# A hybrid encoder block on one core: mixer modulation in sets 1024 columns wide, one gate set placed earlier

## The chip, the cores and the metric

One core of a Trainium2 chip runs the whole layer in one launch. The metric is device time in microseconds: 1252.6 is the median of 3 runs of the kernel before (1247.02 to 1254.28).

## The reference, cut to what matters

256 tokens of width 2048 pass through one layer, all in float32. c is a single vector.

```python
c_act = silu(c)
mod = c_act @ ada_w + ada_b              # 2048 x 12288, one row
shift_a, scale_a, gate_a, shift_f, scale_f, gate_f = split(mod, 6)
h = rmsnorm(x, norm1_w) * (1.0 + scale_a) + shift_a
proj = h @ w_in                          # 2048 x 5184
q_r, k_r, v_r, g_r, cq, ckv, k_rope = split(proj, ...)
# retention heads from q_r, k_r (rotary), v_r, gated by silu(g_r)
# attention heads from the latents cq, ckv (w_uq, w_ukv) and k_rope (rotary)
x = x + gate_a * (concatenate([ret_out, mla_out]) @ w_o)
h = rmsnorm(x, norm2_w) * (1.0 + scale_f) + shift_f
x = x + gate_f * ((silu(h @ w_gate) * (h @ w_up)) @ w_down)
return rmsnorm(x, final_norm_w)
```

## The kernel before

**Weights.** All weight matrices lie in one DRAM stream, cut into loads in the order in which they are used, mostly [128 x 1024] float32 (512 KB). SP issues every DMA. A load lands in a staging slot: the ring `stg` has 6, and until the attention tiles are opened (`att_open`) a second ring `stgx` in the pool `early` adds `DEEP` = 9. A weight load is then split (`split_weights`): ScalarE casts it to `whi` (L126), DVE subtracts to get `wlo` (L128), each with 3 buffers. PE multiplies three times per tile (L134 to L136): high by high, high by low, low by high.

**Modulation.** `ada_set(sec, k0, nk, rowdst, on_pe)` computes nk x 128 columns of one of the six sections. Its loads are staged like weights but not split. On DVE each 128 rows of c are one multiply-add into `ada_acc` (L220; the first is a plain multiply, L218); on PE they are small matmuls (L216). When a set is done, `finish` adds the gate's bias row to row 0 of `ada_acc` (L228 to L232; the row is fetched by its own DMA into a slot of `stg`), and `spread` either broadcasts a gate section over the partitions (ones matrix times `ada_acc`, L238, copied by ScalarE, L239) or transposes a shift or scale section into columns of `mod` (L242 to L250). In the kernel before a set is at most 512 columns, so that a DVE load holds two 512-wide row blocks: two operations per load.

**Order of the work.** A list `steps` is written out and `run` walks it, staging loads ahead. First come four feature groups of the input projection (`GROUPS`: features 0-1, 2-5, 6-9 and 10-15, each 128 wide): while one group is multiplied (`project`, 22 weight steps), the shift and scale sets of the next one are placed evenly between its steps (`ada_stream`, `ADA_PE` says which of them run on PE), and near its end `build_h1` makes the next group's activations, by way of two `hfull` buffers. The last group is mixed with the latents, attention and retention in the list `plan`, and the output projection. Between its entries a planner places the modulation of the mixer's gate and of the first half of the ffn's scale and shift: 8 sets on DVE, 64 loads. It adds up costs by a table and puts in a unit whenever DVE's and the queue's share lags PE's. Then the ffn begins: the first halves of the gate and up projections (features 0-7, `K_LATE`) of the first chunks run while the second half of the ffn's modulation (`units_h`, 25 units) is computed, three units to four half steps; `N_SPILL` = 7 gate chunks leave their half sums in SBUF (`spill`).

**Rotary tables.** `rotary_rows` loads positions and frequencies, `rotary_tables` computes sines and cosines on DVE and ScalarE with the buffers `ang` and `turns`; `kr_rope` is the first to read them (`sc_t`).

The Tile framework derives semaphores and assigns buffers; it also fixes each engine's order by a plan of its own, with the order of the program as the priority, so an engine's order need not be that of the list.

Of the kernel before, what the change touches and what calls it, by code (L numbers as in the profile page):

```python
# [16 lines left out]
P = 128  # L17
T = 256
# [22 lines left out]
GROUPS = [(0, 2), (2, 4), (6, 4), (10, 6)]  # L41
ADA_PE = "10010100101101"
LEAD = [1, 1, 3, 3, 3, 3, 3]
ADA_PE2 = "00000000"
ADA_END = 0.95
LOOK = 3
DEEP = 9
FILL_A = [2, 2]
FILL_M = [3, 0, 1, 0, 4, 2, 1, 3, 2, 2]
FILL_R = [0, 1, 0, 1, 0, 1, 2, 2, 2, 0, 0, 1]  # L50
# [1 line left out]
F_MORE = 2  # L52
F_END = 1
K_LATE = 8
N_SPILL = 7
URGENT = ("finish", "spread", "build_h2", "build_h1")
PE_DELAY = 1
DVE_DELAY = 2
# [26 lines left out]
def encoder_block(ctx: ExitStack, tc: tile.TileContext, x, cols, rows, pos, stream, out):  # L85
# [108 lines left out]
    def ada_set(sec, k0, nk, rowdst, on_pe):  # L194
        n = nk * P
        wide = n if not on_pe else min(n, 2 * P)
        kk = 1024 // wide
        acc = {}

        def acc_tile():  # L200
            return wp.tile([P, n], F32, name="ada_acc", tag="ada_acc", bufs=2, padded_shape=[P, 512])

        def load(c, t, ring):
            w = ring([P, kk, wide])
            SY.dma_start(w.rearrange("p k n -> p (k n)"), stream.take("ada_w", t * kk, kk, sec * D + k0 * P + c, wide))
            return w

        def body(c, t, w):
            if c == 0 and t == 0:
                acc["t"] = bank() if on_pe else acc_tile()  # L210
            a = acc["t"]
            for j in range(kk):
                k = t * kk + j
                if on_pe:
                    q = 32 * (k % 4)
                    PE.matmul(a[q:q + 32, c:c + wide], lhsT=c_pad[:, k], rhs=w[:, j], start=c == 0 and k < 4, stop=c + wide == n and k >= KT - 4)  # L216
                elif k == 0:
                    V.tensor_scalar(out=a, in0=w[:, j], scalar1=c_act[:, 0:1], scalar2=None, op0=ALU.mult)  # L218
                else:
                    V.scalar_tensor_tensor(out=a, in0=w[:, j], scalar=c_act[:, k:k + 1], in1=a, op0=ALU.mult, op1=ALU.add)  # L220

        def finish():
            a = acc["t"]
            if on_pe:
                b, a = a, acc_tile()
                S.copy(a, b[:, 0:n])
            acc["a"] = a
            if rowdst is not None:  # L228
                r0 = (R_GA if sec == GT_A else R_GF) + k0 * P
                br = wp.tile([1, n], F32, name="bias_row", tag="stg", bufs=6)  # L230
                SY.dma_start(br, rows[:, r0:r0 + n])
                V.tensor_tensor(a[0:1, :], a[0:1, :], br, op=ALU.add)  # L232

        def spread():
            a = acc["a"]
            b = bank()
            if rowdst is not None:
                PE.matmul(b[:, 0:n], lhsT=ones, rhs=a, start=True, stop=True)  # L238
                S.copy(rowdst()[:, k0 * P:k0 * P + n], b[:, 0:n])  # L239
                return  # L240
            for j in range(nk):
                PE.transpose(b[:, j * P:(j + 1) * P], a[:, j * P:(j + 1) * P], ident)  # L242
            ks = slice(sec * KT + k0, sec * KT + k0 + nk)
            m = mod[:, ks]
            parts = b[:, 0:n].rearrange("p (j q) -> p j q", q=P)
            V.tensor_reduce(out=m, in_=parts[:, :, ::32] if on_pe else parts, axis=AX.X, op=ALU.add)  # L246
            V.tensor_tensor(m, m, col[:, C_ADAB + ks.start:C_ADAB + ks.stop], op=ALU.add)
            if sec in (SC_A, SC_F):
                g, nw = (gain_a, C_N1) if sec == SC_A else (gain_f, C_N2)
                V.scalar_tensor_tensor(out=g[:, k0:k0 + nk], in0=m, scalar=1.0, in1=col[:, nw + k0:nw + k0 + nk], op0=ALU.add, op1=ALU.mult)  # L250

        loads = [
            ("a", lambda ring, c=c, t=t: load(c, t, ring), lambda w, c=c, t=t: body(c, t, w)) for c in range(0, n, wide) for t in range(KT // kk)
        ]
        return loads, [f(finish), f(spread)]
# [21 lines left out]
    def att_open():  # L277
        early["cm"].__exit__(None, None, None)
        at.cm = tc.tile_pool(name="att", bufs=1)
        at.pool = at.cm.__enter__()  # L280
        at.gate_a = at.pool.tile([P, D], F32, name="gate_a")
        at.krd = at.pool.tile([P, NB, 2, 64], F32, name="krd")
        at.krT = at.pool.tile([P, 2, T], F32, name="krT")
        at.qrT = at.pool.tile([P, 4, T], F32, name="qrT")
# [40 lines left out]

    def rotary_rows():
        SY.dma_start(post, pos)
        SY.dma_start(freq, rows[:, R_FREQ:R_FREQ + 96].partition_broadcast(P))

    def rotary_tables():  # L330
        V.tensor_copy(posf, post)
        for tb in range(NB):
            a = mid.tile([P, 96], F32, name="ang", tag="ang", bufs=2)
            n = mid.tile([P, 96], F32, name="turns", tag="turns", bufs=2)
            V.tensor_scalar(out=a, in0=freq, scalar1=posf[:, tb:tb + 1], scalar2=None, op0=ALU.mult)
            for magic in (1.5 * 2.0 ** 34, 1.5 * 2.0 ** 23):
                V.tensor_scalar(out=n, in0=a, scalar1=1.0 / TWO_PI, scalar2=magic, op0=ALU.mult, op1=ALU.add)
# [20 lines left out]


    pacc = {n: mid.tile([P, NB, 1024], F32, name=f"acc_{n}") for n in "qkvg"}  # L360
    pacc["cq"] = mid.tile([P, NB, 512], F32, name="acc_cq")
    pacc["ck"] = mid.tile([P, NB, 576], F32, name="acc_ck")
    h1 = {}
# [46 lines left out]
    for gi, (k0, nk) in enumerate(GROUPS[:-1]):  # L410
        g0, gn_ = GROUPS[gi + 1]
        units = ada_stream([
            (sec, k, min(4, g0 + gn_ - k), None, ADA_PE[2 * gi + i] == "1") for k in range(g0, g0 + gn_, 4) for i, sec in enumerate((SC_A, SH_A))
        ])
        chunks = WIDE if nk == 1 else CHUNKS
        ws = [w for c in chunks for w in project(gi, *c)]
        lead = len(ws) - LEAD[gi]
# [1 line left out]
        for i, w in enumerate(ws):  # L419
# [8 lines left out]
                steps.append(f(turn_x, 2 * (i + 1)))  # L428
            if gi == 0 and i == len(ws) - 1:
                steps += [f(turn_x, k) for k in range(2 * len(ws) + 2, KT, 2)]  # L430
        if gi:
            steps.append(f((rotary_rows, rotary_tables)[gi - 1]))
    last = len(GROUPS) - 1


# [265 lines left out]
    def out_proj(k0):  # L701
        def chunk(n):
# [3 lines left out]
            def evac(tb, o):  # L706
# [6 lines left out]
                SY.dma_start(xc, x[tb * P:(tb + 1) * P, cs])  # L713
                d = x2[tb][:, cs]
                V.tensor_tensor(d, d, o, op=ALU.add)
                V.tensor_tensor(d, d, at.gate_a[:, cs], op=ALU.mult)
                V.tensor_tensor(d, d, xc, op=ALU.add)
                sq = at.pool.tile([P, 512], F32, name="sq5", tag="sq5", bufs=2)
                S.activation(sq, d, AF.Square, accum_out=stat[:, 20 + 4 * tb + n:21 + 4 * tb + n])
# [101 lines left out]
            plan.append(f(turn_x2, n - 1))  # L821
        plan += c[2:]

    sets = [(GT_A, 4 * i, 4, lambda: at.gate_a) for i in range(4)]
    sets += [(sec, k, min(4, K_LATE - k), None) for sec in (SC_F, SH_F) for k in range(0, K_LATE, 4)]
    units = ada_stream([(*st, on == "1") for st, on in zip(sets, ADA_PE2)])


    work = {
# [11 lines left out]

    costs = [cost(s) for s in plan]
    tot = [sum(c) for c in zip(*costs)]
    share = (len(units) * 1.49 + tot[1], len(units) * 0.524 + tot[2])
    done = [0.0, 0.0, 0.0]
    for s, c in zip(plan, costs):
        steps.append(s)
        done = [a + b for a, b in zip(done, c)]
        if units and done[1] / share[0] + done[2] / share[1] < 2 * done[0] / (tot[0] * ADA_END):
            steps += units.pop(0)  # L850
            done[1] += 1.49
            done[2] += 0.524
    for u in units:
        steps += u

    def gate_f_tile():
        late["gate_f"] = big.tile([P, D], F32, name="gate_f", tag="m8")

    h_late = [(sec, k, 4, None) for k in range(K_LATE, KT, 4) for sec in (SC_F, SH_F)]
    loads, ends_h = ada_set(*h_late[0], True)  # L860
# [82 lines left out]
    def half_step(w):  # L943
        nonlocal count
        steps.append(w)
        count += 1
        if count % 4 and units_h:
            steps.extend(units_h.pop(0))

    for kp in range(0, K_LATE, 2):  # L950
# [6 lines left out]
            ends_h = []  # L957
        if kp == K_LATE - 4:
            steps += [f(scale_x2, K_LATE, 4), f(scale_x2, K_LATE + 4, 4), f(ffn_tiles), f(sg_tile)]
    for j in range(2, N_SPILL + 1):  # L960
        for w in gs[j][:half]:
            half_step(w)
# [117 lines left out]
```

## Time and profile before

| | |
|---|---|
| median of 3 runs | 1252.6 us |
| profiled execution | 1253.46 us |
| its span, first to last instruction | 1251.3 us |
| PE busy | 1202.0 us, 96% |
| DVE busy | 876.9 us, 70% |
| ScalarE (ACT) busy | 602.3 us, 48% |
| mean granted TensorE clock | 0.991 |
| read from DRAM | 312.11 MB |

Busy time is the union of an engine's instructions. A matmul record reaches from issue to its modelled end, so neighbouring records overlap, and a PE that shows as busy may still be waiting a little between them. "Idle before" names what released an engine; L126 is line 126 of the kernel.

### The profile page before, as it was taken

What the parts mean: (1) busy time and instruction counts of PE and PEld (TensorE: products, weight loads), DVE (VectorE), ACT (ScalarE), POOL (GpSimd) and SP (SyncE); (2) the same over time, 40 slices, a digit from 0 to 9 for tenths busy, and PEclk for the clock granted to TensorE, in tenths of its full rate; (3) what the DMA queues carried; (4) which work ended last, traced back from release to release, by engine and by line L of the source; (5) the groups of instructions that cost most, each with busy time, mean ns of one, the idle gap of its engine ahead of it and who ended that gap; (6) DMA issues with size and microseconds to landing.
All of it is one profiled execution on the core that took longest, in us unless ns stands there. A gap on an engine that the chain in (4) does not pass through costs nothing.

```text
span 1251.3 us, 15907 instructions
## 1 busy us (share of the span) xinstructions
PE 1202.0 (96%) x5830; PEld 970.4 (78%) x5830; DVE 876.9 (70%) x1217; ACT 602.3 (48%) x821; POOL 2.2 (0%) x10
## 2 busy tenths in 40 slices
PE   5999999989999999899999999999999999999997
PEld 2676767868888877688888888888888888888885
DVE  2596988998999986988566666655565555655544
ACT  4563443735557754654744444444444443444433
POOL 0000000000000000000000000000000000000000
PEclk8999999999999999999999999999999999999999
DMA  9998897587986786899577667667766676766562
GB/s 379 402 322 302 316 347 256 185 293 262 297 290 212 247 298 211 306 344 334 221 223 225 218 214 211 220 221 222 226 218 218 239 255 213 230 222 204 185 201 85
DMA packets 88797, 315.24 MB, mean 252 GB/s; under 512 B 10248, under 2 KB 10376, under 8 KB 88208
## 3 DMA queue, kind: packets, MB, share of 16 engines
q1 hardware_dynamic: 88720, 314.24, 73.5%
q8 instruction: 45, 0.74, 0.2%
q14 instruction: 32, 0.26, 0.1%
HBM read 312.11 MB, written 2.10 MB: 251 GB/s over the span
## 4 chain that ended last, share of the span: by engine, by line
PE 74%; DVE 11%; DMA 8%; ACT 3%; issue 3%; SPq 0%; ACTq 0%; DVEq 0%
PE bank L135 23%; PE bank L136 23%; PE bank L134 23%; DMA stg<-in_stream 6%; DVE wlo L128 4%; DVE ada_acc L220 3%; DMA stgx<-in_stream 2%; ACT whi L126 1%; PE bank L150 1%; PE bank L216 1%; DMA xt<-in_x 1%; PE bank L238 1%; PE bank L242 0%; ACT hfull L145 0%; PE bank L142 0%
## 5 line engine op out<-in xcount | busy, mean ns | idle before, releaser
L128 DVE TENSOR_TENSOR wlo<-stg,whi 128x1024 fp32r<-128x1024 f32 (+1 forms) x359 | 434.2, 1212 | 260.7 <-ACT whi L126 259.0
L126 ACT CAST whi<-stg 128x1024 fp32r<-128x1024 f32 (+1 forms) x359 | 374.7, 1045 | 478.5 <-PE bank L136 384.6
L134 PE MATMUL bank<-whi,actt 128*128 128x512 f32 (+1 forms) x1184 | 458.4, 393 | 12.3 <-ACT whi L126 9.1
L135 PE MATMUL bank<-wlo,actt 128*128 128x512 f32 (+1 forms) x1184 | 460.3, 389 | 6.6 <-DVE wlo L128 6.3
L136 PE MATMUL bank<-whi,actt 128*128 128x512 f32 (+1 forms) x1184 | 457.1, 386 | 0.2 <-DVE actt L147 0.2
L134 PEld LDWEIGHTS bank<-whi,actt 128*128 128x128 f32 x1184 | 221.5, 188 | 63.3 <-ACT whi L126 11.8
L135 PEld LDWEIGHTS bank<-wlo,actt 128*128 128x128 f32 x1184 | 223.2, 189 | 59.5 <-DVE wlo L128 16.2
L136 PEld LDWEIGHTS bank<-whi,actt 128*128 128x128 f32 x1184 | 223.0, 188 | 44.2 <-DVE actt L147 0.6
L220 DVE SCALAR_TENSOR_TENSOR ada_acc<-stg,c_act,ada_acc 128x512 f32<-128x512 f32 (+1 forms) x243 | 178.9, 737 | 30.1 <-DMA stg<-in_stream 27.4
L134 PE MATMUL bank<-whi,ap 128*128 128x512 f32 x352 | 137.9, 392 | 0.0
L136 PE MATMUL bank<-whi,ap 128*128 128x512 f32 x352 | 137.0, 389 | 0.0
L135 PE MATMUL bank<-wlo,ap 128*128 128x512 f32 x352 | 136.9, 389 | 0.0
L135 PEld LDWEIGHTS bank<-wlo,ap 128*128 128x128 f32 x352 | 66.1, 188 | 14.2 <-issue 0.5
L134 PEld LDWEIGHTS bank<-whi,ap 128*128 128x128 f32 x352 | 66.1, 188 | 14.1 <-issue 0.5
L136 PEld LDWEIGHTS bank<-whi,ap 128*128 128x128 f32 x352 | 66.1, 188 | 13.6
L126 ACT CAST whi<-stgx 128x1024 fp32r<-128x1024 f32 (+1 forms) x41 | 37.7, 928 | 43.9 <-PE bank L136 31.1
L128 DVE TENSOR_TENSOR wlo<-stgx,whi 128x1024 fp32r<-128x1024 f32 (+1 forms) x41 | 43.7, 1073 | 18.5 <-ACT whi L126 12.1
L216 PE MATMUL bank<-stg,c_pad 128*32 128x256 f32 x200 | 17.8, 416 | 12.7 <-DMA stg<-in_stream 12.6
L220 DVE SCALAR_TENSOR_TENSOR ada_acc<-stgx,c_act,ada_acc 128x512 f32<-128x512 f32 (+1 forms) x42 | 29.5, 703 | 0.6
L216 PEld LDWEIGHTS bank<-stg,c_pad 128*32 128x32 f32 x200 | 5.2, 112 | 22.1 <-issue 14.4
L147 DVE TENSOR_TENSOR actt<-hfull,actt 128x256 fp32r<-128x256 f32 x40 | 16.2, 418 | 2.3 <-ACT actt L146 1.7
L246 DVE TENSOR_REDUCE mod<-bank 128x4 f32<-128x512 f32 (+3 forms) x18 | 8.5, 470 | 9.8 <-PE bank L242 9.7
(227 smaller groups left out, 786.6 us busy)
## 6 DMA issues: line engine op xcount, KB each, us to landing
stg<-in_stream SPq DMA_DIRECT2D x500, 512.0 KB, 4.5
stgx<-in_stream SPq DMA_DIRECT2D x68, 512.0 KB, 6.8
stgx<-in_stream SPq DMA_DIRECT2D x13, 288.0 KB, 3.7
stg<-in_stream SPq DMA_DIRECT2D x8, 384.0 KB, 3.6
xt<-in_x SPq DMA_DIRECT2D x2, 1024.0 KB, 6.5
acc_cq<-in_x SPq DMA_DIRECT2D x8, 256.0 KB, 4.9
out<-x SPq DMA_DIRECT2D x8, 256.0 KB, 3.3
acc_k<-in_rows SPq DMA_DIRECT2D x1, 1024.0 KB, 4.7
```

Source lines behind the costliest of these rows:

```text
L126: S.copy(hi, stg)
L128: V.tensor_tensor(lo, stg, hi.bitcast(F32), op=ALU.subtract)
L134: PE.matmul(o, lhsT=ah, rhs=whi, start=first, stop=False)
L135: PE.matmul(o, lhsT=ah, rhs=wlo, start=False, stop=False)
L136: PE.matmul(o, lhsT=al, rhs=whi, start=False, stop=last)
L147: V.tensor_tensor(dst[:, k, T:2 * T], tmp, dst[:, k, 0:T].bitcast(F32), op=ALU.subtract)
L150: PE.transpose(b[:, j, tb * P:(tb + 1) * P], src, ident)
L216: PE.matmul(a[q:q + 32, c:c + wide], lhsT=c_pad[:, k], rhs=w[:, j], start=c == 0 and k < 4, stop=c + wide == n and k >= KT - 4)
L220: V.scalar_tensor_tensor(out=a, in0=w[:, j], scalar=c_act[:, k:k + 1], in1=a, op0=ALU.mult, op1=ALU.add)
L238: PE.matmul(b[:, 0:n], lhsT=ones, rhs=a, start=True, stop=True)
L246: V.tensor_reduce(out=m, in_=parts[:, :, ::32] if on_pe else parts, axis=AX.X, op=ALU.add)
```

## The change

Gate set 0 (columns 0 to 511 of gate_a) is computed in the second feature group instead of after the fourth has begun. The remaining mixer sets become 512 columns (gate, 4 to 7), 1024 (gate, 8 to 15), 1024 (ffn scale) and 1024 (ffn shift): 56 loads, of which 48 hold one 1024-wide row block. `spread` goes over a wide set in parts of 512. The bias row of a whole gate is loaded once into row 0 of the gate's tile, and `finish` adds from there. `gate_a` moves from the attention pool to the pool `mid`; so does `ada_acc`, until the ffn pool is open. To make room, `DEEP` goes from 9 to 7, and the rotary tables take their buffers from `hfull`. `rotary_rows` runs behind the first group. Modulation loads in the ffn start only once the ffn pool is open (after nine half steps), and `N_SPILL` goes to 9.

```diff
-ADA_PE2 = "00000000"
-DEEP = 9
+DEEP = 7
-N_SPILL = 7
+N_SPILL = 9
         def acc_tile():
-            return wp.tile([P, n], F32, name="ada_acc", tag="ada_acc", bufs=2, padded_shape=[P, 512])
+            wide = [P, 512 if "pool" in late else 1024]
+            return late.get("pool", mid).tile([P, n], F32, name="ada_acc", tag="ada_acc", bufs=2, padded_shape=wide)
             if rowdst is not None:
-                r0 = (R_GA if sec == GT_A else R_GF) + k0 * P
-                br = wp.tile([1, n], F32, name="bias_row", tag="stg", bufs=6)
-                SY.dma_start(br, rows[:, r0:r0 + n])
-                V.tensor_tensor(a[0:1, :], a[0:1, :], br, op=ALU.add)
+                V.tensor_tensor(a[0:1, :], a[0:1, :], rowdst()[0:1, k0 * P:k0 * P + n], op=ALU.add)
         def spread():
-            a = acc["a"]
+            for j in range(0, nk, 4):
+                spread_part(k0 + j, min(4, nk - j), acc["a"][:, j * P:])
+        def spread_part(k0, nk, a):
+            n = nk * P
             b = bank()
             if rowdst is not None:
-                PE.matmul(b[:, 0:n], lhsT=ones, rhs=a, start=True, stop=True)
+                PE.matmul(b[:, 0:n], lhsT=ones, rhs=a[:, 0:n], start=True, stop=True)
                 S.copy(rowdst()[:, k0 * P:k0 * P + n], b[:, 0:n])
...
-        at.gate_a = at.pool.tile([P, D], F32, name="gate_a")
+    gate_a = mid.tile([P, D], F32, name="gate_a")
     def rotary_rows():
         SY.dma_start(post, pos)
+        SY.dma_start(gate_a[0:1, :], rows[:, R_GA:R_GA + D])
...
-            a = mid.tile([P, 96], F32, name="ang", tag="ang", bufs=2)
-            n = mid.tile([P, 96], F32, name="turns", tag="turns", bufs=2)
+            a = mid.tile([P, 96], F32, name="ang", tag="hfull", bufs=2, padded_shape=[P, T])
+            n = mid.tile([P, 96], F32, name="turns", tag="hfull", bufs=2, padded_shape=[P, T])
...
         units = ada_stream([
             (sec, k, min(4, g0 + gn_ - k), None, ADA_PE[2 * gi + i] == "1") for k in range(g0, g0 + gn_, 4) for i, sec in enumerate((SC_A, SH_A))
-        ])
+        ] + [(GT_A, 0, 4, lambda: gate_a, False)] * (gi == 1))
-        if gi:
-            steps.append(f((rotary_rows, rotary_tables)[gi - 1]))
+        if gi != 1:
+            steps.append(f((rotary_rows, rotary_tables)[gi // 2]))
...
-    sets = [(GT_A, 4 * i, 4, lambda: at.gate_a) for i in range(4)]
-    sets += [(sec, k, min(4, K_LATE - k), None) for sec in (SC_F, SH_F) for k in range(0, K_LATE, 4)]
-    units = ada_stream([(*st, on == "1") for st, on in zip(sets, ADA_PE2)])
+    units = ada_stream([(sec, k, n, (lambda: gate_a) if sec == GT_A else None, False) for sec, k, n in (
+        (GT_A, 4, 4), (GT_A, 8, 8), (SC_F, 0, K_LATE), (SH_F, 0, K_LATE),
+    )])
-    share = (len(units) * 1.49 + tot[1], len(units) * 0.524 + tot[2])
+    share = (len(units) * 1.3 + tot[1], len(units) * 0.524 + tot[2])
-            done[1] += 1.49
+            done[1] += 1.3
     def gate_f_tile():
         late["gate_f"] = big.tile([P, D], F32, name="gate_f", tag="m8")
+        SY.dma_start(late["gate_f"][0:1, :], rows[:, R_GF:R_GF + D])
...
-        if count % 4 and units_h:
+        if "pool_open" in late and count % 4 and units_h:
             steps.extend(units_h.pop(0))
...
             steps += [f(scale_x2, K_LATE, 4), f(scale_x2, K_LATE + 4, 4), f(ffn_tiles), f(sg_tile)]
+            late["pool_open"] = True
```

## Rows read from the trace of the kernel before

**Rows 1.** Busy time by engine, the page's part 1

```profile
PE 1202.0 (96%) x5830; PEld 970.4 (78%) x5830; DVE 876.9 (70%) x1217; ACT 602.3 (48%) x821; POOL 2.2 (0%) x10
```

**Rows 2.** Stretches: PE, PEld, DVE, ACT, POOL busy us, PEclk, DMA share, GB/s

```profile
0.00:75.00 75.00, 53.66 (x318) 33.98 (x319) 35.61 (x54) 42.34 (x67) 1.31 (x8) 0.95 0.96 373
75.00:140.00 65.00, 64.43 (x342) 48.95 (x341) 52.72 (x75) 26.94 (x33) 0.00 (x0) 1.00 0.86 312
205.00:240.00 35.00, 34.85 (x200) 30.54 (x199) 34.38 (x67) 20.71 (x41) 0.93 (x2) 1.00 0.61 192
240.00:460.00 220.00, 209.24 (x1113) 174.78 (x1113) 209.06 (x371) 128.55 (x227) 0.00 (x0) 0.98 0.79 268
500.00:530.00 30.00, 25.60 (x111) 19.89 (x111) 27.80 (x40) 18.22 (x27) 0.00 (x0) 0.94 0.82 300
530.00:640.00 110.00, 110.00 (x494) 90.26 (x493) 79.53 (x94) 60.61 (x76) 0.00 (x0) 1.00 0.82 293
640.00:1235.00 595.00, 595.00 (x2658) 491.92 (x2657) 348.94 (x354) 253.50 (x274) 0.00 (x0) 1.00 0.66 214
```

**Rows 3.** Waits from 240 to 460 us: total us, times, longest

```profile
ACT whi L126 <- DMA stg<-in_stream: 46.9, 28, 5.1
ACT whi L126 <- PE bank L136: 11.6, 8, 2.2
```

**Rows 4.** Timeline of ScalarE in the second feature group

```profile
89.50 1.05 ACT L126 CAST whi<-stgx 128x1024 fp32r<-128x1024 f32 x1 [1.67 <-PE bank L136]
92.22 1.05 ACT L126 CAST whi<-stgx 128x1024 fp32r<-128x1024 f32 x1 [1.67 <-PE bank L136]
...
121.92 1.05 ACT L126 CAST whi<-stgx 128x1024 fp32r<-128x1024 f32 x1 [2.47 <-DVE acc_k L388]
125.44 1.05 ACT L126 CAST whi<-stgx 128x1024 fp32r<-128x1024 f32 x1 [2.47 <-PE bank L136]
```

**Rows 5.** Instructions that touch ada_acc: ns min/median/max, first to last start, forms

```profile
L220 DVE SCALAR_TENSOR_TENSOR ada_acc<-stgx,c_act,ada_acc x42: 477/745/754, 46.7 to 223.2; 128x512 f32<-128x512 f32 x35, 128x256 f32<-128x256 f32 x7
...
L218 DVE TENSOR_SCALAR ada_acc<-stg,c_act x15: 445/481/487, 204.3 to 1008.2; 128x512 f32<-128x512 f32 x15
```

**Rows 6.** Timeline of DVE, 340 to 349 us: start, us

```profile
340.04 2.32 DVE L220 SCALAR_TENSOR_TENSOR ada_acc<-stg,c_act,ada_acc 128x512 f32<-128x512 f32 x3
...
344.51 0.74 DVE L220 SCALAR_TENSOR_TENSOR ada_acc<-stg,c_act,ada_acc 128x512 f32<-128x512 f32 x1
345.17 0.16 DVE L550 TENSOR_SCALAR st<-st 128x2 f32<-128x2 f32 x1
...
347.39 1.28 DVE L388 TENSOR_TENSOR acc_q<-acc_q,bank 128x512 f32<-128x512 f32 x2
348.58 1.22 DVE L128 TENSOR_TENSOR wlo<-stg,whi 128x1024 fp32r<-128x1024 f32 x1
```

**Rows 7.** Waits of SP's queue, whole span: total us, times, longest

```profile
SPq L231 <- DVE wlo L128: 7.5, 5, 2.3
...
SPq L231 <- DVE lat_ck L147: 2.3, 1, 2.3
```

**Rows 8.** Timeline of DVE: first table operation, last hfull reads of the third build_h1

```profile
143.73 0.16 DVE L331 CAST posf<-post 128x2 f32<-128x2 int32 x1
...
203.68 0.75 DVE L147 TENSOR_TENSOR actt<-hfull,actt 128x256 fp32r<-128x256 f32 x2
```

**Rows 9.** Instructions that touch sc_t: ns min/median/max, first to last start

```profile
L345 DVE TENSOR_SCALAR sc_t<-ang x2: 204/206/209, 162.6 to 166.4; 128x96 f32<-128x96 f32 x2
L355 DVE TENSOR_TENSOR krd<-acc_ck,sc_t x2: 216/216/217, 226.9 to 227.1; 128x64 f32<-128x64 f32 x2
...
L346 ACT ACTIVATE sc_t<-sc_t x1: 526/526/526, 166.7 to 166.7; 128x384 f32<-128x384 f32 x1
```

**Rows 10.** Costly DVE groups from 500 to 530 us: busy us, mean ns

```profile
L220 DVE SCALAR_TENSOR_TENSOR ada_acc<-stg,c_act,ada_acc 128x512 f32<-128x512 f32 x13 | 9.7, 748 | 0.4 <-DMA stg<-in_stream 0.2
```

More of the change, by code (lines that the diff above doesn't have):

```diff
@@ L715, in evac @@
                 V.tensor_tensor(d, d, o, op=ALU.add)
-                V.tensor_tensor(d, d, at.gate_a[:, cs], op=ALU.mult)
+                V.tensor_tensor(d, d, gate_a[:, cs], op=ALU.mult)
                 V.tensor_tensor(d, d, xc, op=ALU.add)
```

## The prediction

> **What bounds the kernel now.** I read the busy shares first [rows 1]: PE 96% of the span, DVE 70%. An average says little here, so I cut the span into stretches that follow the stages [rows 2]. From 530 to 1235 us (gate, up and down projections) PE is busy without a gap, while DVE has 349 of 595 us of work: nothing on DVE or in the DMA queue can shorten that part, and whatever is won before 530 us comes out at the end unchanged. The other half is different. From 240 to 460 us (last projection group, attention, retention, first half of the output projection) DVE has 209.06 of 220 us of work and PE shows 10.8 us without any matmul; as matmul records overlap, PE's true slack is larger than that. ScalarE's casts there wait for the weight load to land (46.9 us, 28 times) and less for PE (11.6 us) [rows 3]: staging slots come free only when DVE has read them, so a late DVE shows up as a late load. I take this stretch as DVE-bound. From 75 to 140 us it is the other way round: DVE 52.72 of 65, PE 64.43, and the casts start every 2.72 or 3.52 us, released by PE's matmuls or by the DVE addition that empties their banks [rows 4].
>
> **Part 1: 1024-wide sets.** Of the 64 modulation loads that run beside the mixer, 8 move away (part 2), 8 stay 512 wide, and 48 become 1024 wide: one DVE operation per load where there were two. Three of the 48 are the first of a set (a plain multiply), 45 are multiply-adds. A 256-wide multiply-add takes 477 ns and a 512-wide one 745 [rows 5], so 256 columns add 268 ns, and a 1024-wide one would take 745 + 2 x 268 = 1281 ns (an estimate; the trace has none). What counts is the distance to the next start: 0.66 us behind a lone 512-wide one (344.51 to 345.17, so 0.08 less than its length), and in a back-to-back run of three, 2.32 us long, (2.32 - 0.745) / 2 = 0.79 us [rows 6], since each reads what the one before wrote. So a pair costs 1.32 to 1.45 us, a single wide one 1.28 - 0.08 = 1.20: a saving of 0.12 to 0.25 each, 5.4 to 11.3 us for 45; I take 0.19, 8.6 us, as both patterns are frequent. The three multiplies I leave at their cost. The bias additions cost the same per column as before.
>
> The Trainium skill (VectorE: DVE Perf Modes, the section on the TRN2 errata) gives VectorE a fixed 58 cycles per SBUF operation beside one column a cycle, that is 60 ns saved per fold, and 45 folds would give an estimated 2.7 us instead of 8.6; by it the forecast would be some 4 us later, the stretch giving 13 x 14.2 / 20.1 = 9 us. The trace does not agree: starts 0.66 us apart less 2 x 0.268 us of columns leave 0.12 us per operation, twice that, so the measured rows stand.
>
> **Part 2: the first gate set moves.** 16 DVE operations and a bias addition leave the DVE-bound stretch: 15 multiply-adds at 0.70 (the middle of the two distances), the first multiply at 0.48 - 0.08 and an addition over 512 columns at 0.60, 11.5 us. They go into the second feature group (about 75 to 140 us), with their 8 DMAs of 512 KB on SP's queue, one matmul against the ones matrix and one ScalarE copy. That group then places 25 units over 21 weight steps instead of 17, so 1.19 per step for 0.81. While DVE units run, a step costs DVE 1.14 (the split) + 0.64 (two accumulator adds, 1.28 us, every second step; both from [rows 6]) + 1.19 x 1.45 = 3.5 us against the 2.72 of PE [rows 4]; today it is 2.96. Over the first third (6.7 steps) that is 5 us lost where now some 2.4 are; the last third enters behind the PE-side set with up to three split tiles in hand (8 us of PE work), which covers its 5 us. Net +4 us, bounds 0 (all in today's 12 us of DVE idle) and 11.5 (none). Loads: 20.3 MB in 65 us now [rows 2], 24.5 MB in 69 us then, 355 GB/s, below the 373 that the first 75 us moved.
>
> **What the 240 to 460 us stretch gives back.** DVE loses 8.6 + 11.5 = 20.1 us there. Ends of the range: 20.1 if DVE set the pace throughout, 0 if the loads do. PE's visible gaps of 10.8 us are the nearest row; with some room beyond them I take 13. What is late next is PE.
>
> **Part 3: bias rows.** A bias row took a slot of the six-slot staging ring and a place in SP's queue; most of what its eight issues waited for slots is 7.5 + 2.3 us [rows 7]. Four of them lie before 460 us. Removing them: 0 to 3 us, I take 1; the four behind lie under PE. The two 8 KB row loads that replace them go straight to gate_a and gate_f.
>
> **Part 4: rotary tables.** They now share the two-slot hfull ring. Today their chain runs from 143.7 to 166.6 us, in the midst of the third group, although the program lists it behind that group [rows 8, 9]; so the order on DVE is planned, not the program's. If it has to wait for the third build_h1 (last read of hfull at 203.7 us), 32 operations of 0.20 to 0.26 us, some 7 us of DVE, land in 205 to 240 us, where DVE has 34.38 of 35 [rows 2]. If the slots are taken early, nothing changes. 0 to +7, I take 1, since position rows arrive a group earlier.
>
> **Part 5: entry to the ffn.** Modulation loads now start after nine half steps instead of with the first, so 7 units, 14 DVE operations, 10 us, leave 503 to 530 us (13 multiply-adds, DVE 27.80 of 30, PE idle 4.4, [rows 2, 10]) for the stretch behind, where DVE idles 30.5 of 110 us. The normalisation that opens this stretch holds PE too and stays. Gain 0 to 4.4, I take 2. Two more spilled chunks add four ScalarE copies and four DVE adds, under PE; if that cover were gone, some 5 us.
>
> **Part 6: shallower early ring.** 13 slots instead of 15 while the first 75 us move 373 GB/s: at most two loads late, 2 x 512 KB at that rate, 2.8 us; I take 0.5, since it costs only where the ring has run dry.
>
> **Sum** against the profiled execution (1253.5 us, span 1251.3): -13 + 4 - 1 + 1 - 2 + 0.5 = -10.5, so 1243.0. The median shown is 0.9 lower than that execution, so 1242.
>
> **Rivals.** (a) The loads become the bound: the 46.9 us of casts waiting for landings [rows 3] would stay, since six slots remain. Then the stretch gives 6 instead of 13: 1249. Against it: SP itself mostly waits there for slots that DVE frees. Also 1249 if the wide operation costs as much as two halves. (b) DVE gives everything back and the moved set is free: 1253.5 - 20.1 - 1 + 1 - 2 + 0.5 - 0.9 = 1231. For it: DVE's share of 95%. Against: PE shows only 10.8 us of gaps to close. (c) Slower: the rotary chain behind hfull. It took 22.9 us (143.7 to 166.6), and the sine 0.5; started at 204.4 it ends at 227.8, past 226.9, when the rotary key first reads the table [rows 8, 9], and it holds both slots that the latents' splits need. With all of these 23.4 us exposed: 1253.5 - 10.5 + 23.4 - 0.9 = 1265.5. It turns the sign from 10.5 us of exposed delay on.
>
> **Chances.** Forecast 0.51 (own range 1234 to 1248), rival (a) 0.25, (b) 0.14, (c) 0.10. Within 0.5% (6.3 us, about what a measurement can tell) means 1246.3 to 1258.9. Faster: 0.44 of the forecast's 0.51, 0.14 of (b), 0.08 of (a), 0.66. Slower: 0.09 of (c). Same: 0.25. The range 1229 to 1257 leaves out the far part of (b) and most of (c).
>
> **What would show it.** In the changed trace: 45 multiply-adds of 1024 columns at about 1.28 us; DVE still over 90% busy between 240 us and the output projection, and that stretch 13 us shorter; the second group some 4 us longer, its casts more often held by DVE; PE idle between entry and 530 us smaller. Wrong: the second group longer by over 10 us, PE gaps before the up-projections with the sine late, or casts waiting for loads as long as now in a stretch that hasn't shrunk.

## The result, and the profile after

The changed kernel takes 1267.03 us (median of 4 runs, 1264.35 to 1267.58) against 1253.44 us for the kernel before on the same chip: a ratio of 1.011, 95% interval 1.0076 to 1.0144. It is slower by 13.6 us, where 10.5 less was forecast. The profiled execution took 1267.58 us, its span is 1265.8.

First, where in the program the time lies. A stage begins where its first instruction starts, so rows that list the instructions on one tile with their first and last start give the marks. The first adds into `acc_cq` open the second and the third feature group (the six run over groups 2 to 4); the first `x<-x,gate_a` is the first use of the mixer's gate; `rstd_b` opens the ffn. Kernel before (the second row lists only what starts from 100 to 200 us):

```profile
L388 DVE TENSOR_TENSOR acc_cq<-acc_cq,bank x6: 679/686/689, 77.0 to 215.2; 128x512 f32<-128x512 f32 x6
L388 DVE TENSOR_TENSOR acc_cq<-acc_cq,bank x2: 686/686/686, 141.0 to 141.7; 128x512 f32<-128x512 f32 x2
L716 DVE TENSOR_TENSOR x<-x,gate_a x8: 677/684/694, 459.4 to 494.3; 128x512 f32<-128x512 f32 x8
L759 ACT COPY rstd_b<-bank x1: 372/372/372, 500.1 to 500.1; 128x256 f32<-128x256 f32 x1
```

The changed kernel:

```profile
L390 DVE TENSOR_TENSOR acc_cq<-acc_cq,bank x6: 679/680/689, 76.4 to 235.2; 128x512 f32<-128x512 f32 x6
L390 DVE TENSOR_TENSOR acc_cq<-acc_cq,bank x2: 680/680/680, 156.0 to 156.6; 128x512 f32<-128x512 f32 x2
L718 DVE TENSOR_TENSOR x<-x,gate_a x8: 683/684/692, 474.0 to 509.6; 128x512 f32<-128x512 f32 x8
L761 ACT COPY rstd_b<-bank x1: 373/373/373, 515.7 to 515.7; 128x256 f32<-128x256 f32 x1
L347 ACT ACTIVATE sc_t<-sc_t x1: 522/522/522, 254.6 to 254.6; 128x384 f32<-128x384 f32 x1
```

The second group is 156.0 - 76.4 = 79.6 us long where it was 141.0 - 77.0 = 64.0: 15.6 more. The fourth opens one add (0.7 us) ahead of the last start, so the third group took 78.5 for 73.6, 4.9 more. From there to the first gate multiply it was 244.8 and is 239.5: 5.3 given back. To `rstd_b` it is 41.7 for 40.7, and behind it nothing changed (750.1 for 751.2). The sine, last step of the rotary tables, starts at 254.6 where it started at 166.7 [rows 9].

The stretches that answer to [rows 2], changed kernel, same columns:

```profile
75.00:140.00 65.00, 58.95 (x289) 41.48 (x288) 47.48 (x69) 22.87 (x29) 0.00 (x0) 0.92 0.84 300
140.00:205.00 65.00, 59.22 (x298) 41.46 (x297) 52.70 (x83) 22.38 (x29) 0.00 (x0) 0.97 0.88 312
240.00:460.00 220.00, 211.11 (x1155) 181.51 (x1154) 205.47 (x357) 140.16 (x255) 0.95 (x2) 0.98 0.76 258
```

From 75 to 140 us PE lost 5.5 us of busy time, DVE 5.2, and the granted clock fell from 1.00 to 0.92. Over the second group from mark to mark PE stands idle for 7.2 us of 79.6, where it was 0.6 of 64.0, and DVE for 17.9, where it was 12.1. Both engines were emptier in a longer stage: they waited for each other in turn.

### The profile page after: what moved, and what is told of

It is laid out like the page before. It is cut to its first block, busy times and chain, and to the rows that moved or that the text cites. A ratio compares the mean times of both kernels' runs of the same rounds, so it can differ in the third digit from the quotient of the medians.

```text
span 1265.8 us, 15848 instructions
## 1 busy us (share of the span) xinstructions
PE 1211.4 (96%) x5830; PEld 976.8 (77%) x5830; DVE 873.3 (69%) x1172; ACT 606.2 (48%) x826; POOL 2.3 (0%) x10
## 4 chain that ended last, share of the span: by engine, by line
PE 75%; DVE 11%; DMA 7%; issue 3%; ACT 2%; SPq 0%; ACTq 0%; DVEq 0%
PE bank L134 24%; PE bank L135 23%; PE bank L133 23%; DMA stg<-in_stream 5%; DVE wlo L127 4%; DVE ada_acc L220 3%; DMA stgx<-in_stream 2%; PE bank L216 2%; PE bank L149 2%; ACT whi L125 1%; PE bank L658 1%; PE bank L243 0%; ACT hfull L144 0%; PE bank L647 0%; PE bank L239 0%
## 5 line engine op out<-in xcount | busy, mean ns | idle before, releaser
L125 ACT CAST whi<-stg 128x1024 fp32r<-128x1024 f32 (+2 forms) x365 | 379.6, 1041 | 500.1 <-PE bank L135 455.3
L127 DVE TENSOR_TENSOR wlo<-stg,whi 128x1024 fp32r<-128x1024 f32 (+2 forms) x365 | 439.8, 1208 | 257.7 <-ACT whi L125 256.0
L220 DVE SCALAR_TENSOR_TENSOR ada_acc<-stg,c_act,ada_acc 128x512 f32<-128x512 f32 (+1 forms) x188 | 164.7, 876 | 39.7 <-DMA stg<-in_stream 37.5
L125 ACT CAST whi<-stgx 128x1024 fp32r<-128x1024 f32 (+1 forms) x35 | 33.2, 949 | 32.4 <-PE bank L135 29.5
L127 DVE TENSOR_TENSOR wlo<-stgx,whi 128x1024 fp32r<-128x1024 f32 (+1 forms) x35 | 38.4, 1102 | 8.7 <-ACT whi L125 8.0
L220 DVE SCALAR_TENSOR_TENSOR ada_acc<-stgx,c_act,ada_acc 128x512 f32<-128x512 f32 (+1 forms) x52 | 34.9, 671 | 0.7
L216 PE MATMUL bank<-stg,c_pad 128*32 128x256 f32 x216 | 20.7, 443 | 12.3 <-DMA stg<-in_stream 12.2
L216 PEld LDWEIGHTS bank<-stg,c_pad 128*32 128x32 f32 x216 | 5.4, 115 | 23.3 <-issue 15.1
L146 DVE TENSOR_TENSOR actt<-hfull,actt 128x256 fp32r<-128x256 f32 x40 | 16.5, 420 | 6.0 <-ACT actt L145 4.7
```

The costliest lines, as they stand in the source:

```text
L125: S.copy(hi, stg)
L127: V.tensor_tensor(lo, stg, hi.bitcast(F32), op=ALU.subtract)
L146: V.tensor_tensor(dst[:, k, T:2 * T], tmp, dst[:, k, 0:T].bitcast(F32), op=ALU.subtract)
```

## Inside the second group

Three marks cut the group in three parts, called thirds here although the last is longer: the first adds into `acc_q` and `acc_g`, and the group's end. Before, then changed:

```profile
L388 DVE TENSOR_TENSOR acc_q<-acc_q,bank x12: 678/679/689, 89.4 to 348.0; 128x512 f32<-128x512 f32 x12
L388 DVE TENSOR_TENSOR acc_g<-acc_g,bank x12: 676/679/686, 107.6 to 378.2; 128x512 f32<-128x512 f32 x12
```

```profile
L390 DVE TENSOR_TENSOR acc_q<-acc_q,bank x12: 668/682/689, 97.4 to 361.5; 128x512 f32<-128x512 f32 x12
L390 DVE TENSOR_TENSOR acc_g<-acc_g,bank x12: 668/680/689, 121.1 to 393.5; 128x512 f32<-128x512 f32 x12
```

From the group's start to `acc_q`: 12.4 us before, 21.0 after, 8.6 lost. From there to `acc_g`: 18.2 and 23.7, 5.5 lost. From there to the end: 33.4 and 34.9, 1.5 lost. The first third in steps of 5 us; before (columns as [rows 2]):

```profile
80.00:85.00 5.00, 5.00 (x37) 4.79 (x36) 5.00 (x10) 3.06 (x3) 0.00 (x0) 1.00 0.90 325
85.00:90.00 5.00, 5.00 (x24) 4.14 (x23) 4.93 (x7) 1.66 (x3) 0.00 (x0) 1.00 0.91 332
```

and changed (the last row lies in the last third):

```profile
80.00:85.00 5.00, 2.62 (x20) 2.38 (x19) 4.93 (x9) 2.10 (x2) 0.00 (x0) 1.00 0.91 303
85.00:90.00 5.00, 3.37 (x12) 2.56 (x11) 4.89 (x9) 1.04 (x1) 0.00 (x0) 0.50 0.98 377
90.00:95.00 5.00, 5.00 (x13) 3.25 (x14) 1.70 (x2) 1.04 (x1) 0.00 (x0) 0.50 1.00 396
135.00:150.00 15.00, 13.84 (x58) 9.87 (x56) 15.00 (x21) 5.63 (x6) 0.00 (x0) 1.00 0.78 268
```

DVE was already full before (5.00 and 4.93 of 5), with PE just fed. Now DVE is as full and PE gets half. The timeline of DVE shows in what order it works (start, us):

```profile
80.58 0.75 DVE L220 SCALAR_TENSOR_TENSOR ada_acc<-stg,c_act,ada_acc 128x512 f32<-128x512 f32 x1
...
81.36 2.33 DVE L220 SCALAR_TENSOR_TENSOR ada_acc<-stg,c_act,ada_acc 128x512 f32<-128x512 f32 x3
83.60 0.75 DVE L127 TENSOR_TENSOR wlo<-stgx,whi 128x576 fp32r<-128x576 f32 x1
84.27 2.32 DVE L220 SCALAR_TENSOR_TENSOR ada_acc<-stgx,c_act,ada_acc 128x512 f32<-128x512 f32 x3
...
97.38 0.69 DVE L390 TENSOR_TENSOR acc_q<-acc_q,bank 128x512 f32<-128x512 f32 x1 [5.67 <-PE bank L135]
```

A split (L127) stands behind three or four multiply-adds, and PE waits for it: 2.38 us at 84.41 and 1.63 at 89.17. These first steps carry 576 columns, not 1024, so PE is through one in 1.6 us (the distance of their casts before) and not 2.72, while the units are spread evenly by the number of steps. Then the roles change: by 97 us DVE has been idle 5.67 us for PE, whose matmuls now come at half their rate, as the chain of waits has them (start, us, what):

```profile
89.17 0.79 PE bank L134
89.97 0.43 PE bank L135
...
96.18 0.23 PE bank L134
```

The same 512-column matmul takes 0.43 us from 89.97 on and 0.23 at 96.18: the granted clock was 0.50 (1.2 of 2.4 GHz) from 85 to 95 us, after the 2.38 us in which PE had nothing. The 12 of them that start from 89.97 to 95.52 lost 0.20 each, 2.4 of the 8.6 us.

The middle third loses its 5.5 us on PE. The small matmuls of the sets that PE computes (L216), before (those past 141.0 belong to the third group) and after:

```profile
L216 PE MATMUL bank<-stgx,c_pad x56: 379/391/403, 101.1 to 151.7; 128*32 128x256 f32 x56
```

```profile
L216 PE MATMUL bank<-stgx,c_pad x40: 379/379/636, 94.6 to 121.9; 128*32 128x256 f32 x40
L216 PE MATMUL bank<-stg,c_pad x24: 379/391/403, 99.2 to 109.9; 128*32 128x256 f32 x24
```

With 25 units over the group that set is pressed into 94.6 to 121.9. The middle third by itself, L216 alone (us from and to, length, PE busy, PEld busy, PEclk, DMA share, GB/s), before and after:

```profile
89.40:107.60 18.20, 1.28 (x16) 0.32 (x16) 1.00 0.95 362
97.40:121.10 23.70, 5.48 (x54) 1.46 (x54) 1.00 0.82 279
```

That is 4.2 of the 5.5 us. The set leaves the last third, but PE can't use the room there: from 135 to 150 us DVE, with the moved set, is busy 15.00 of 15.

## The experiments

The ratio is to the kernel before, run in turn with it on the same chip; that kernel's own median moved from 1251.1 to 1253.4 us between such groups of runs, so differences between two rows of the table are good to some 2 us. "Second group" and "mixer" are lengths in us by the marks above (the mixer from the fourth group's first add to the first gate multiply), "sine" is its start.

| run | median us | ratio, 95% | second group | mixer | sine |
|---|---|---|---|---|---|
| before | 1253.44 | | 64.0 | 244.8 | 166.7 |
| after | 1267.03 | 1.0076 to 1.0144 | 79.6 | 239.5 | 254.6 |
| a_stay | 1248.33 | 0.9965 to 0.9991 | 66.2 | 241.1 | 237.8 |
| a_ang | 1265.42 | 1.0086 to 1.0138 | 81.1 | 236.2 | 104.8 |
| b_move | 1262.22 | 1.0070 to 1.0119 | 86.4 | 235.3 | 172.8 |
| b_deep7 | 1250.78 | 0.9979 to 1.0026 | 64.0 | 242.8 | 166.4 |
| a_mix | 1253.36 | 0.9995 to 1.0025 | 70.1 | 238.9 | 242.5 |
| a_pe | 1267.12 | 1.0096 to 1.0132 | 80.8 | 239.6 | 255.0 |
| a_stay_ang | 1243.75 | 0.9915 to 0.9944 | 69.3 | 231.6 | 110.1 |
| b_wide_e | 1240.81 | 0.9889 to 0.9925 | 64.0 | 234.0 | 168.6 |
| b_entry | 1250.31 | 0.9975 to 1.0004 | 64.0 | 245.2 | 165.7 |
| a_stay_narrow | 1262.94 | 1.0060 to 1.0108 | 66.2 | 252.7 | 237.6 |
| a_stay_narrow_ang | 1256.41 | 1.0025 to 1.0060 | 69.1 | 246.5 | 110.6 |
| a_mix_ang (a_mix again) | 1253.79 | 0.9991 to 1.0021 | 70.1 | 238.9 | 243.6 |
| a_mix_ownring | 1254.44 | 1.0001 to 1.0029 | 75.0 | 236.1 | 100.0 |

**a_stay**, gate set 0 back behind the fourth group:

```diff
-        ] + [(GT_A, 0, 4, lambda: gate_a, False)] * (gi == 1))
+        ])
-        (GT_A, 4, 4), (GT_A, 8, 8), (SC_F, 0, K_LATE), (SH_F, 0, K_LATE),
+        (GT_A, 0, 4), (GT_A, 4, 4), (GT_A, 8, 8), (SC_F, 0, K_LATE), (SH_F, 0, K_LATE),
```

> The changed kernel with one thing undone: gate set 0 stays in the plan behind the fourth group (first of the sets there). Theory 1 (the moved set crowds the second feature group: PE starves, the granted clock halves for some 10 us, and DVE is the bound in the last third): the second group is back from 79.6 to about 64 us, the stretch behind pays up to 11 us for the returned set, total 1253 to 1258. Theory 2 (rotary tables late through the hfull ring): the second group may shorten, but the total stays at 1262 to 1268. Theory 3 (early ring of 13 slots): second group still over 75 us, total 1265 or more.

18.7 us come back (16.5 by the ratios); 13.4 us in the second group and 4.3 in the third. The mixer, with the set back in it, is only 1.6 longer, where theory 1 allowed up to 11; so the kernel is faster than any of the three theories had it. The moved set makes the loss.

**a_ang**, the rotary tables in a two-slot ring of their own:

```diff
-            a = mid.tile([P, 96], F32, name="ang", tag="hfull", bufs=2, padded_shape=[P, T])
-            n = mid.tile([P, 96], F32, name="turns", tag="hfull", bufs=2, padded_shape=[P, T])
+            a = mid.tile([P, 96], F32, name="ang", tag="ang", bufs=2)
+            n = mid.tile([P, 96], F32, name="turns", tag="ang", bufs=2)
```

> The changed kernel, but the rotary tables' two temporaries have a two-slot ring of their own instead of hfull. Theory 1: sine at about 165 us instead of 254, total 1261 to 1267 (at most 6 us better), second group still near 79 us. Theory 2: total 1250 to 1256. Theory 3: no change, 1265 to 1268.

The sine is 150 us earlier and the time stays. The late sine is not what made the change slower.

**b_move**, the kernel before with the moved set alone (`gate_a` in `mid` and 13 early slots, which it needs):

```diff
-DEEP = 9
+DEEP = 7
...
+        ] + [(GT_A, 0, 4, lambda: gate_a, False)] * (gi == 1))
...
-    sets = [(GT_A, 4 * i, 4, lambda: at.gate_a) for i in range(4)]
+    sets = [(GT_A, 4 * i, 4, lambda: gate_a) for i in range(1, 4)]
```

> The kernel before with gate_a in the pool mid, the early ring 7 deep and gate set 0 moved into the second group, nothing else (sets 512 wide, bias rows as before, rotary temporaries their own). Theory 1: second group near 79 us instead of 64, total 1260 to 1268. Theory 2: second group near 68 us, total 1248 to 1254. Theory 3: as slow as the kernel before with the ring 7 deep alone.

The move alone costs the kernel before about 11 us: the second group takes 22.4 more, the third 4.6 less, and the mixer, 235.3 for 244.8, gives 9.5 back. The first two thirds of the second group lose 5.7 and 5.5 us, the middle one as in the changed kernel, and the last loses 11.2. What is new is at the end of the group, as its waits from 140 to 156 us and two windows show:

```profile
PE bank L238 <- DVE ada_acc L232: 8.5, 1, 8.5
```

```profile
145.00:150.00 5.00, 0.00 (x0) 0.00 (x0) 4.86 (x8) 0.00 (x0) 0.00 (x0) 0.77 0.96 353
150.00:155.00 5.00, 3.19 (x6) 1.86 (x7) 4.86 (x14) 0.59 (x1) 0.00 (x0) 0.50 0.43 147
```

PE's order holds the ones matmul of the gate (L238), which waits for the last DVE addition of the set; all matmuls stand behind it. In the changed kernel that wait is small (1.1 us).

**b_deep7**, the kernel before with `DEEP = 7` alone.

> The kernel before with the early ring 7 deep instead of 9, nothing else. Theories 1 and 2: 1252 to 1256. Theory 3: 1260 to 1268, with the loss between 75 and 235 us.

No difference. The shallower ring is out as a cause.

**a_mix**, the changed kernel with the same 25 units in the second group, but alternated DVE, PE, DVE:

```diff
-        ] + [(GT_A, 0, 4, lambda: gate_a, False)] * (gi == 1))
+        ])
+        if gi == 1:
+            sets = [(sec, g0, gn_, None, pe) for sec, pe in ((SC_A, False), (SH_A, True))]
+            on_dve, on_pe = ada_stream([sets[0], (GT_A, 0, 4, lambda: gate_a, False)]), ada_stream([sets[1]])
+            units = [u for i in range(len(on_pe)) for u in on_dve[2 * i:2 * i + 1] + on_pe[i:i + 1] + on_dve[2 * i + 1:2 * i + 2]]
```

> The changed kernel with the same 25 units in the second group, but the 16 DVE units (scale set, then the moved gate set) and the 8 PE units laid alternately, two to one, instead of eight DVE, eight PE, eight DVE. Theory 1a (the loss is crowding: DVE units in a row outrun DVE, PE empties and its clock falls): second group 66 to 72 us instead of 79.6, total 1254 to 1261. Theory 1b (the loss is the amount of work in that group, however placed): second group 76 us or more, total 1263 to 1268.

13.7 us come back (12.5 by the ratios) with the same units and the same loads. Its first third, columns as before:

```profile
80.00:85.00 5.00, 4.17 (x33) 3.26 (x31) 4.93 (x10) 2.05 (x3) 0.00 (x0) 1.00 1.00 392
85.00:90.00 5.00, 4.32 (x25) 2.95 (x24) 4.10 (x6) 1.73 (x2) 0.00 (x0) 1.00 0.97 368
```

PE is never starved as far as in the changed kernel and the clock stays at 1.00, as theory 1a had it. So it is not the number of loads or slots that makes most of the loss, but how densely DVE's units stand against short weight steps. Of the group's 9.5 us that come back the first third has 5.8, the middle one 0.6 and the last 3.1. 6.1 us of the group's cost remain: 2.8 in the first third and 4.9 in the middle one, less 1.6 in the last. In the middle third L216 now takes 2.53 us and PE stands idle for 2.45 of 23.1, so the pressed PE set is not all that makes that third long; the rest of its cost is open.

**a_pe**, the moved set on PE instead of DVE:

```diff
-        ] + [(GT_A, 0, 4, lambda: gate_a, False)] * (gi == 1))
+        ] + [(GT_A, 0, 4, lambda: gate_a, True)] * (gi == 1))
```

> The changed kernel with the moved gate set computed on PE (32 small matmuls) instead of DVE, in the same place. Theory 1 (DVE is what the moved set overloads): second group 68 to 74 us, as 8 more PE units cost PE about 1 us each and DVE nothing; total 1255 to 1262. Rival (its loads and staging slots are the cost): second group stays near 79 us, total 1264 to 1268.

A miss: 80.8 us where 68 to 74 was expected. I had placed the loss in the last third, where DVE was full; with the set on PE the last third is PE-bound instead (15.00 busy of 15 from 120 to 135 us), and the first third is unchanged:

```profile
80.00:85.00 5.00, 2.62 (x20) 2.38 (x19) 4.89 (x10) 2.10 (x2) 0.00 (x0) 1.00 1.00 350
```

This is what sent me to the first third: what crowds it is not the moved set's own work (that comes last) but the scale set's DVE units, placed 1.19 per step now for 0.81.

**a_stay_ang**, the edits of a_stay and of a_ang together.

> Gate set 0 back in the plan as in the run before, and the rotary temporaries in a two-slot ring of their own. The sine should come near 105 to 170 us instead of 238. If the late sine costs what the forecast's part 4 allowed (up to 7 us), 1241 to 1246; if it is hidden, 1247 to 1250.

With the moved set gone the early sine is worth 4.6 us (9.5 in the mixer, 3.1 lost in the second group, into which the tables' DVE work comes).

**b_wide_e**, the kernel before with the sets 1024 wide, `DEEP` left at 9, no moved set, the rotary tables in one ring of their own, the planner's new cost, and the new ffn entry:

```diff
...
-            n = mid.tile([P, 96], F32, name="turns", tag="turns", bufs=2)
+            n = mid.tile([P, 96], F32, name="turns", tag="ang", bufs=2)
-    sets = [(GT_A, 4 * i, 4, lambda: at.gate_a) for i in range(4)]
-    sets += [(sec, k, min(4, K_LATE - k), None) for sec in (SC_F, SH_F) for k in range(0, K_LATE, 4)]
+    sets = [(GT_A, 8 * i, 8, lambda: at.gate_a) for i in range(2)]
+    sets += [(sec, 0, K_LATE, None) for sec in (SC_F, SH_F)]
...
```

> The kernel before with the wide sets (gate 8 + 8, ffn scale 8, ffn shift 8) and the later start of the ffn's modulation with 9 spilled chunks; gate set 0 in the plan, early ring 9 deep, bias rows by their own loads, rotary temporaries in one ring of their own. If the wide sets and the ffn entry are the useful parts: 1240 to 1247. If the narrower ring and the bias rows of the changed kernel matter too: 1247 to 1252.

1240.81 us: faster than both kernels, by 0.75% to 1.11% than before. The second group keeps its 64.0 us, and the mixer gives 10.8.

**b_entry**, the kernel before with the new ffn entry alone:

```diff
-N_SPILL = 7
+N_SPILL = 9
-        if count % 4 and units_h:
+        if "pool_open" in late and count % 4 and units_h:
+            late["pool_open"] = True
```

> The kernel before with the ffn entry of the change alone: modulation loads of the ffn start after nine half steps, and nine gate chunks are spilled. By the prediction's step (7 units, 14 DVE operations, leave the opening of the ffn, where PE idled 4.4 us) it is 0 to 4.4 us faster, about 1249, with the stretch from the normalisation to the first ffn products shorter. The rival says that PE is held there by the normalisation and the gap stays: within 1 us of before, about 1251.5, the extra spills lying under PE. If the spills are not hidden, up to 5 us slower.

The rival holds: 0.7 us, inside the interval. It also prices the wide sets in b_wide_e, with the planner's cost and the one ring: 1250.31 - 1240.81 = 9.5 us.

**a_stay_narrow**, a_stay with every mixer set 512 wide and the planner's old cost:

```diff
-        (GT_A, 0, 4), (GT_A, 4, 4), (GT_A, 8, 8), (SC_F, 0, K_LATE), (SH_F, 0, K_LATE),
+        (GT_A, 0, 4), (GT_A, 4, 4), (GT_A, 8, 4), (GT_A, 12, 4), (SC_F, 0, 4), (SC_F, 4, 4), (SH_F, 0, 4), (SH_F, 4, 4),
-    share = (len(units) * 1.3 + tot[1], len(units) * 0.524 + tot[2])
+    share = (len(units) * 1.49 + tot[1], len(units) * 0.524 + tot[2])
...
```

> The changed kernel with gate set 0 back behind the fourth group, and every mixer set 512 columns wide again: all else stays, the late sine too. If the wide sets are worth what the prediction's first step says (8.6 us of DVE time in a stretch that DVE bounds), it is 5 to 9 us slower than the kernel with the wide sets (1248.3), so 1253 to 1257, the growth in the stretch from the fourth group to the first gate multiply. The rival says that with PE as the next bound the width gives nothing back: within 2 us of 1248.

14.6 us slower than a_stay, beyond the 5 to 9 expected. The whole stretch from the fourth group to the first gate multiply in a_stay_narrow, in a_stay, and in the changed kernel (columns as [rows 2]):

```profile
217.00:470.00 253.00, 235.95 (x1269) 198.73 (x1268) 237.61 (x449) 148.95 (x266) 0.94 (x2) 0.98 0.75 256
```

```profile
217.00:459.00 242.00, 231.94 (x1268) 198.59 (x1267) 230.90 (x401) 149.78 (x266) 0.93 (x2) 0.98 0.79 272
```

```profile
234.00:474.00 240.00, 231.11 (x1265) 199.03 (x1264) 220.28 (x384) 148.88 (x265) 0.95 (x2) 0.98 0.75 255
```

Width takes 6.7 us of DVE work out, and PE's gap falls from 17.1 to 10.1 us. Moving the set takes 10.6 more from DVE, and PE's gap only goes to 8.9.

**a_stay_narrow_ang**, the same with the rotary tables in their own ring.

> The kernel with gate set 0 back behind the fourth group and every mixer set 512 wide, and now with the rotary tables in a two-slot ring of their own, so that the sine is early. That kernel was 11.9 us above before with the sine at 237.6 us, its loss in the stretch from the fourth group to the first gate multiply (252.7 us for 244.8). If the late sine makes that loss, this one is 8 to 12 us faster: 1251 to 1255, the stretch back near 245. The rival puts the loss on the other parts (the shared ring of 13 slots, the gate tile, the order of the loads): then no more than the 4.6 us that the early sine gave with wide sets, 1258 or more.

6.5 us, between the two: less than the 8 to 12 of the theory, more than the rival's 4.6. What is left above before, 4.3 us, lies mostly in the second group (69.1 for 64.0), where the tables' DVE work now falls. Against a_stay_ang (1243.75) it prices the wide sets a third time: 12.7 us.

**a_mix_ang** is a_mix once more: its rotary tables still share the ring of `hfull`. Its expectation is for a kernel with a ring of their own, and it does not test it:

> The changed kernel with the moved set and its neighbours interleaved DVE, PE, DVE as in the interleaved run, and with the rotary tables in a two-slot ring of their own. If the two faults, bunched DVE work in the second group and the late sine, add up, it is 4 to 6 us faster than the interleaved run (1253.4): 1247 to 1250, the sine near 105 us, the second group near 70 us. If the moved set relieves the stretch behind the fourth group at all, it also beats the kernel with the set left in place and the early sine (1243.75); I expect that it does not, since the second group keeps about 4 us of its cost and DVE's relief was 1 to 2 us.

As a repeat it says that a_mix stands: 1253.79 us after 1253.36.

**a_mix_ownring** is the kernel that was meant.

> The interleaved kernel (moved set and its neighbours DVE, PE, DVE) with the rotary tables in a two-slot ring of their own. The run labelled for this before used the shared ring by mistake and so repeated the interleaved kernel (1253.8 after 1253.4). If the two faults, bunched DVE work in the second group and the late sine, add up, this is 4 to 6 us faster than that: 1248 to 1250, the sine near 105 us. If the moved set relieves the stretch behind the fourth group at all, it also beats the kernel with the set left in place and the early sine (1243.75); I expect that it does not.

The sine is at 100.0 as expected, but the time stays at 1254.44: the two faults do not add up. The mixer gains 2.8 us and the second group loses 4.9: the tables' work is one more thing for DVE there, PE is busy 2.15 of 5 us from 80 to 85 us, and the clock is 0.50 from 85 to 90. And the moved set does not pay: the same kernel with the set left in place (a_stay_ang) takes 1243.75.

## Why the prediction was wrong

**The step that failed is Part 2, "Net +4 us, bounds 0 (all in today's 12 us of DVE idle) and 11.5 (none)".** It measured +15.6 in the second group, above its upper bound, and the third group adds 4.9. By a_stay 0.6 of that is due to the rest of the change; of the 4.3, only this is known: from 156 to 205 us PE waits 4.6 us for splits, where from 141 to 190 us it waited 1.8 before, and the clock is 0.83 from 165 to 175 us. The profiled executions put 25.0 us between forecast (-10.5) and result (+14.5): Part 2 makes 11.6 of them, the third group 4.9 and the mixer 7.7. The working itself came to 5 less 2.4, 2.6 us; what raised it to 4 was not said. Three things were missing in it. It took the first third by an average step of 2.72 us, the pace of 1024-column casts [rows 4], where the first steps are 576 columns wide and pass in about 1.6; DVE was busy 9.93 of 10 us there before and had no margin. It priced a late DVE by DVE's time alone, and not by the clock that PE loses after it stands empty. And it looked at the first and last thirds, on DVE, and not at the middle one, into which PE's own set is pressed. The last third, for which the cover by split tiles was invoked, lost 1.5 us only. The bound of 11.5 treated the moved work as the whole price; in fact most of the cost falls on units that were there before and now stand closer.

**"240–460 gives back 13"** gave 5.3, from three terms, each taken from one pair of runs. The wide sets gave 11.6 (a_stay_narrow to a_stay). The late sine took 6.2 to 9.5 (the narrow and the wide pair). The moved set gave 1.6 (a_stay to after) of the 11.5 us of DVE work that it took away. The terms depend on one another. With narrow sets the same move gave 9.5 (before to b_move). With wide sets and the early sine it took 4.6 (a_stay_ang to a_ang, 231.6 to 236.2), and with the set moved the late sine takes only 3.3 (a_ang to after). From 244.8 us before, wide sets reach 234.0 without the move (b_wide_e), the move 235.3 without wide sets (b_move), and both, with the early sine, 236.2 (a_ang): together no more than either alone. "What is late next is PE" points the right way, and should have been applied to the second relief. The waits of ScalarE from 240 to 460 us, as [rows 3], in a_stay:

```profile
ACT whi L125 <- PE bank L135: 30.1, 21, 2.6
ACT whi L125 <- DMA stg<-in_stream: 22.6, 8, 4.6
```

and in the changed kernel:

```profile
ACT whi L125 <- PE bank L135: 38.0, 28, 2.6
...
ACT whi L125 <- DMA stg<-in_stream: 6.1, 2, 3.8
```

With narrow sets (a_stay_narrow) the casts waited 51.8 us for loads and 7.2 for PE; the wide sets make it 22.6 and 30.1, the moved set 6.1 and 38.0. So DVE's second relief reached the casts, but they then waited for PE, and PE's gaps in the stretch only went from 10.1 to 8.9 us. What holds PE in those 8.9, and why the move lengthens the mixer where the sine is early, no run here shows.

**Part 1** sized the operation rightly and its worth too low. The 45 multiply-adds of 1024 columns take up to 1286 ns, for 1281 estimated:

```profile
L220 DVE SCALAR_TENSOR_TENSOR ada_acc<-stg,c_act,ada_acc x188: 741/752/1286, 54.0 to 1161.2; 128x512 f32<-128x512 f32 x143, 128x1024 f32<-128x1024 f32 x45
```

Three pairs of runs price the wide sets at 9.5, 12.7 and 14.6 us (10.4, 14.0 and 13.3 by the ratios); DVE's busy time fell by 6.7, for 8.6 predicted. Why the time falls by more than the work is open; the planner's cost and the order of the loads change with the width. The fixed cost in the table of the Trainium skill (VectorE: DVE Perf Modes, the section on the TRN2 errata), 58 cycles or 60 ns, does not agree with this trace: two of 752 ns against one of 1286 make 218 ns. The same section of the Trainium skill says that this row comes out too low and puts the measured fixed term of a copy at about 150 cycles, an estimated 156 ns, which the prediction passed over; the trace is above that too.

**Part 4** (+1, bounds 0 and 7): the tables did wait for the third `build_h1`, as feared (its last read of `hfull` starts at 223.4, the sine at 254.6); with the moved set gone this costs 4.6 to 6.5 us against tables that come in the second group. **Part 5** (-2): 0.7, not to be told from none. **Part 6** (+0.5): none. **Part 3** (-1) was not tried alone; a_stay_ang, which has it along with the shallower ring, the gate's tile in `mid`, two gate sets left 512 wide and the earlier tables, is 2.9 us slower than b_wide_e, which has none of these, so no gain shows.

**The rivals.** (c) named 1265.5, close to the result, but for another reason: its mechanism appears (sine at 254.6), and a_ang shows that taking it away changes the time by 1.6 us, inside the intervals. (a) is refuted: the casts stopped waiting for loads. (b) fails by its premise that the moved set is free, and the mixer gave 5.3 of its 20.1. The line that I gave as a sign of error, the second group longer by over 10 us, is the one that came true; I gave it no chance and no price of its own.

## What to carry to other kernels

Work moved out of a bound stage is worth something only as long as that stage has no other bound close behind (the same move gave the mixer 9.5 us with narrow sets and 1.6 with wide ones), and it must go to where the receiving engine has room in each short window, not on average: cut the receiving stage into 5 us windows and look for engines at 5.00 of 5. Units spread evenly by the count of steps crowd the short steps. Alternating the engines won 13.7 us back; spreading the units by the time that a step takes is the next thing to try, which no run here did. Make each part of a bundled change pay for itself: here the wide sets, with the planner's cost that goes with them, gave 0.8 to 1.2%, and the moved set took that and more.

## What the runs showed of the hardware

A TensorE that stood empty for 2.38 us behind a busy VectorE (TensorE busy 2.62 of 5 us) ran the following 10 us at a granted clock of 0.50, the lower of its two levels (1.2 GHz for 2.4), its 512-column matmul taking 0.43 us for 0.23. By the 12 matmuls counted above the stall cost 2.4 us on top of its length. In a_pe, after the same 2.62 of 5, the clock was 0.52 and 0.80 in the next two windows of 5 us. The run with the same units interleaved (a_mix) was busy at least 4.12 of 5 in every window of the second group and kept 1.00. In b_move the clock is 0.77 and then 0.50 as PE stands empty for 8.5 us.

A float32 multiply-add of VectorE over 1024 columns took up to 1286 ns, two over 512 columns 752 each, so one wide operation is 0.22 us shorter than two narrow ones.
